# Taking four engines' instructions in the planner's order instead of the build tool's

## The chip, the cores and the metric

The kernel runs on one core of a Trainium2 chip. The metric is the time of one execution on the device in microseconds (us); lower is better. A kernel is timed in several runs, and the median of them is its time.

## What is computed

Two layers of a decoder over 1024 tokens of width 1024 in float32. Layer 0 is "forgetting attention" (FoX): a causal softmax attention whose scores carry a running sum of log forget gates. Layer 1 is native sparse attention (NSA): each query attends to compressed blocks of keys, to the key blocks selected (with this size all causal ones), and to a window of 512 keys, and the three results are summed by gates. Its keys and values are made once from the residual stream behind layer 0. Each layer ends with a feed-forward part with a convolution over three tokens. Cut to that:

```python
def conv_ffn(xn, w_up, conv_w, conv_b, w_down):       # width 1024 -> 2 x 2816 -> 1024
    u = xn @ w_up
    u_pad = jnp.pad(u, ((0, 0), (CONV_W - 1, 0), (0, 0)))
    c = sum((conv_w[j] * u_pad[:, j:j + T] for j in range(CONV_W)), conv_b)
    gate, val = jnp.split(c, 2, axis=-1)
    return (jax.nn.silu(gate) * val) @ w_down

def reference(x, positions, ...):
    h = x
    for layer in range(2):
        if layer == 0:
            h = h + forgetting_attention(rms_norm(h, a_norm[0]), a_w_in[0], ..., a_w_out[0])
        else:
            h = h + native_sparse_attention(rms_norm(h, b_norm[0]), positions, kc, vc, ks, vs, kw, vw, b_w_in[0], ...)
        h = h + conv_ffn(rms_norm(h, f_norm[layer]), f_w_up[layer], f_conv_w[layer], f_conv_b[layer], f_w_down[layer])
        if layer == 0:
            kc, vc, ks, vs, kw, vw = shared_kv(h, positions, kv_norm, kv_w, ...)
    return h
```

## The kernel before

**Products.** Every large matmul is made in three passes over operands that are split into a high part (rounded) and a low part (the remainder): high x high, high x low, low x high (`mm3`, L206 to L212, so nearly all matmuls stand under L210, L211 and L212). ScalarE rounds the high part (L1021 in the FFN, L859 and L216 elsewhere) and VectorE subtracts it from the source for the low part (L1022, shown under its helper L1017). The up and down projections of the FFN are each cut in 2 x 2 blocks and made by Strassen's scheme of seven products with sums of blocks before and after, so VectorE also makes `sum`, `xs`, `u` and `b` (L1017 too).

**Task lists.** Five stretches of the kernel are not written as loops of instructions but as lists of tasks: the FoX attention (`fox_attn`), the FFN of layer 0 and of layer 1 (`ffn`, called twice), the entry of the NSA layer, with keys, values and part of the query projection (`nsa_in`), and the NSA attention (`nsa_attn`). A task names an engine, a duration, a priority (a position `u` plus an offset for its kind), what it comes after and which buffers of which ring it takes. `Flow.run` (L147) plays the engines through with those durations: at each step the task that can start first is taken, by priority among those that can, and its function is called, which emits its instructions. So the order of the instructions in the source is the order of that plan. The input projection of layer 0 and a rest of its output projection are no lists; they stand as written.

**What sets the order that runs.** Each engine runs its instructions in one order. In the kernel before, the build tool orders the instructions of every engine anew by costs of its own, within what data and buffers allow; the plan's order is only where it starts from. The transfers are issued by SyncE (SP), whose queue the tool orders too.

**Lines that the following sections name.** Attention: scores `s` by TensorE (L584, L785, L1895, L1896, L1917, L1920), row maximum `sm` by VectorE (L593, L588), exponential `pt` by ScalarE (L596), scaling by GpSimd (L600), transposes `t` by TensorE (L613), the split of `t` into `p_h` (ScalarE, L624) and `p_l` (VectorE, L626), product with the values `v` (L618, L619), results copied and added into `ot` (L638, L642). The compressed branch of the NSA attention has its own softmax: L1924 (maximum), L1936 (VectorE subtracts it), L1940 (ScalarE exponential), L1928 to L1931 and L1941 (GpSimd scales). The output weights of layer 1 are split by `split_tasks`: L859 (ScalarE, high part) and L860 (GpSimd, low part). Query norms: L1668 (square), L1661 (sums), L235 and L236 (root), L239 to L243 (correction of the root), L1429 (scaling), L1401 to L1406 (rotation, GpSimd), L1678 (transposes), L1685 and L1686 (split). L956 is a square for the norm ahead of the second FFN, made inside the NSA attention. FFN: norm by L1042 (square), L1045 (GpSimd), L1053 (transposes), L1057; then the seven products of each of 22 channel blocks, `snap` (L1152), the convolution by L1198 (ScalarE) and two taps L1197 (VectorE), the gated product L1207, and the down projection. Each finished row of the FFN of layer 0 is normed (`leave`, L2106 to L2119, GpSimd's part L2119) for the NSA layer.

**Rotation tables.** `self.rope` holds sine and cosine for the rotation of keys and queries. For the queries the gain is multiplied into them once: `q_turns` makes four tables `turn_q` with four GpSimd products (L1470), as a task of its own with priority 8, early in the list of `nsa_in`.

Of the kernel before, what the change touches and what calls it, by code (L numbers as in the profile page):

```python
# [6 lines left out]
FT = mybir.dt.float32  # L7
# [3 lines left out]
AF = mybir.ActivationFunctionType  # L11
OP = mybir.AluOpType
# [4 lines left out]
P = 128  # L17
T = 1024
D = 1024
NT = T // P  # L20
# [50 lines left out]
class Ring:  # L71
# [9 lines left out]
    def room(self):  # L81

        rooms = [self.n % len(self.rooms)] if self.turn else range(len(self.rooms))
        c = [(b.free + .2 if b else 0.0, k) for k in rooms for b in [self.rooms[k]] if b is None or not b.left]
        return min(c) if c else (None, None)
# [109 lines left out]
class Trunk:  # L195
    def __init__(self, tc, A):
        self.tc, self.nc, self.A = tc, tc.nc, A

    def pool(self, name, bufs=1, side=None, space=None):
        kw = {"space": space} if space is not None else {}  # L200
        if space is not DRAM:
            kw["reuse_waits"] = "tile"
        return self.tc.tile_pool(name=name, bufs=bufs, side=side, **kw)

# [40 lines left out]
    def rstd_tasks(self, ss, n, inv, scale):  # L245

        st = {}

        def begin():
            st["f"], st["r"] = self.rstd_steps(self.ap_o, ss(), n, inv)  # L250
            st["f"][0]()

        def end():
            st["f"][2]()
            scale(st["r"])
        return [("DVE", .08, "Q", begin), ("ACT", .45, "Q", lambda: st["f"][1]()), ("DVE", .9 if n > 1 else 1.4, "Q", end)]
# [482 lines left out]
    def fox_attn(self, qT, kT, vS, xT, weights, w_room, o_late, wo_steps, early):  # L739
        nc, hp = self.nc, self.hp  # L740
        with ExitStack() as es:
# [3 lines left out]
            F = self.flow  # L745
# [8 lines left out]
            u = 0  # L754
# [65 lines left out]
            F.run()  # L820
# [164 lines left out]
    def ffn(self, layer, xT, first, X, U, rows, g_dram, conv, leave, ahead=None):  # L985
# [11 lines left out]
        with ExitStack() as es:  # L997
            en = es.enter_context
            fp = en(self.pool("ff", 1))
            self.ap_o = en(self.pool("ff_sm", 2))  # L1000
# [33 lines left out]
            def norm(i, n):  # L1034
# [5 lines left out]
                def square():  # L1040
                    st["ss"] = self.ap_o.tile([P, 1], FT, name="nt_ss")
                    nc.scalar.activation(xt.t, x.t, AF.Square, accum_out=st["ss"])  # L1042
                load = F.add("SP", moved(P, D), u, "", lambda: nc.sync.dma_start(x.t, rows[i]), (), [x])
                *steps, last = self.rstd_tasks(lambda: st["ss"], 1, 1.0 / D, lambda r: st.update(r=r))
# [299 lines left out]
            F.run()  # L1344
# [78 lines left out]
    def nsa_in(self, turns, begin, quarters, xT, kv, q_dram, nw):  # L1423
# [6 lines left out]
        with ExitStack() as es:  # L1430
# [30 lines left out]
            turn_q = [cc.tile([P, NT, 8], FT, name=f"turn_q{m}") for m in range(4)]  # L1461
# [6 lines left out]
            def q_turns():  # L1468
                for tq, (t, x) in zip(turn_q, ((1, 0), (0, 1), (1, 1), (0, 0))):
                    nc.gpsimd.tensor_tensor(tq, self.rope[t][:, :NT], gr[:, None, 8 * x:8 * x + 8].to_broadcast([P, NT, 8]), op=OP.mult)  # L1470
# [131 lines left out]
            turns_made = F.add("POOL", 1.5, 8, "", q_turns)  # L1602
# [24 lines left out]
            u = 0  # L1627
# [25 lines left out]


# [58 lines left out]
            F.run()  # L1713
# [150 lines left out]
    def nsa_attn(self, kv, q_dram, late, wo, steps, res, dst, norms, nw):  # L1864
# [3 lines left out]
        with ExitStack() as es:  # L1868
# [149 lines left out]
            F.run()  # L2018
# [3 lines left out]
    def kv_tiles(self, p, U):  # L2022
        ku = U(0, [8, 512], "k_u")
        vu = U(1, [2, 4, G, P], "v_u")
        kv = {"k": [[[[p.tile([P, 512], FR, name=f"k{br}{g}{x}"), ku[:, br * 4 + g * 2 + x]] for x in range(2)]
                     for g in range(G)] for br in range(2)]}
        kv["v"] = [[p.tile([P, 4, G, P], FR, name=f"v{br}"), vu[:, br]] for br in range(2)]
        kv["kc"] = p.tile([P, G, 2, HD], FR, name="kc")
        kv["vc"] = [[p.tile([P, P], FR, name=f"vc{g}{a}") for a in range(2)] for g in range(G)]
        kv["gate"] = p.tile([P, NT, 3 * H], FT, name="gate")  # L2030
        return kv

    def build(self, out):
        A, nc = self.A, self.nc
        with self.pool("const", 1) as cp, self.pool("dram", 1, space=DRAM) as dp, self.pool("w", 3) as self.wp, \
# [70 lines left out]
            def leave(F, i, h, after, u):  # L2106
# [7 lines left out]
                def square():  # L2114
                    st["ss"] = self.ap_o.tile([P, 1], FT, name="nt_ss")
                    nc.scalar.activation(junk.t, h(), AF.Square, accum_out=st["ss"])
                *steps, last = self.rstd_tasks(lambda: st["ss"], 1, 1.0 / D, lambda r: st.update(r=r))
# [106 lines left out]
```

## Time and profile before

| what | us |
|---|---|
| median of 3 runs (lowest, highest) | 2728.29 (2725.96, 2731.55) |
| the profiled execution | 2730.28 |
| its span, first to last instruction | 2728.5 |
| TensorE busy (share of the span) | 2643.6 (97%) |
| VectorE busy | 2138.1 (78%) |
| ScalarE busy | 1511.9 (55%) |
| GpSimd busy | 560.8 (21%) |
| mean granted clock of TensorE | 0.994 |

The stages follow one another nearly without overlap: input projection of layer 0 from 0 to 253, FoX attention to 620, rest of its output projection to 657, first FFN to 1310, entry of the NSA layer to 1486, NSA attention to 2076, second FFN to the end. In the rows below PE is TensorE, DVE is VectorE, ACT is ScalarE, POOL is GpSimd. A row of the timeline gives start and duration in us, engine, line, operation, output and inputs by the program's names, and in brackets the time in which the engine stood idle before it with the instruction that released it. Idle time of an engine other than TensorE costs only what it makes TensorE wait.

### The profile page before, as it was taken

The page shows a single profiled execution, that of the slowest core. Times are in us where ns is not written, and L with a number is a line of the kernel's source. Part 1 is how long each engine was busy: PE and PEld are TensorE (multiplying, and loading weights), DVE is VectorE, ACT ScalarE, POOL GpSimd, SP SyncE. Part 2 cuts the span into 40 slices and gives each one's busy share as a digit, 9 for nine tenths or more (in the row PEclk, how much of TensorE's full clock was granted, in tenths as well). Part 3 has the DMA queues.
Part 4 walks back from the last instruction along what each step waited for, and adds up shares of the span by engine and source line. Part 5 has one row for each costly group of instructions (what it writes and reads, how often), then busy time and mean ns, then how long its engine had stood idle before and what let it go on. Part 6 is the DMA issues. An engine that isn't in the chain of part 4 may idle for free. (4 is left out here: it accounts for less than half of the span.)

```text
span 2728.5 us, 39283 instructions
## 1 busy us (share of the span) xinstructions
PE 2643.6 (97%) x13384; PEld 2174.1 (80%) x13384; DVE 2138.1 (78%) x4012; ACT 1511.9 (55%) x3168; POOL 560.8 (21%) x843
## 2 busy tenths in 40 slices
PE   8999999999999999999999899999999999999999
PEld 6678777787788888888888688887787788888887
DVE  6752778755987787989786788887886987877988
ACT  5332677744655454445754677676776554545443
POOL 1111445410000000000463654444452000000000
PEclk9999999999999999999999899999999999999999
DMA  6474657724332224544224300000113422224553
GB/s 183 110 180 160 173 159 208 188 89 135 120 98 72 93 71 147 214 139 156 90 80 136 109 20 17 28 28 32 63 44 112 136 85 93 77 85 165 189 167 128
DMA packets 277209, 312.42 MB, mean 115 GB/s; under 512 B 19992, under 2 KB 194496, under 8 KB 277008
## 3 DMA queue, kind: packets, MB, share of 16 engines
q1 hardware_dynamic: 277008, 309.90, 37.0%
q8 instruction: 106, 1.74, 0.3%
q14 instruction: 95, 0.78, 0.1%
HBM read 238.41 MB, written 71.43 MB: 114 GB/s over the span
## 5 line engine op out<-in xcount | busy, mean ns | idle before, releaser
L1021 ACT CAST op<-sum 128x512 fp32r<-128x512 f32 x396 | 241.7, 622 | 309.9 <-PE ps L212 200.6
L210 PE MATMUL ps<-xs,op 128*128 128x512 f32 x880 | 344.9, 393 | 7.9 <-ACT snap L1152 5.5
L211 PE MATMUL ps<-xs,op 128*128 128x512 f32 x880 | 344.0, 391 | 0.4 <-DVE xs L1017 0.4
L212 PE MATMUL ps<-xs,op 128*128 128x512 f32 x880 | 342.6, 390 | 0.4 <-DVE op L1017 0.4
L596 ACT ACTIVATE pt<-s,sm 128x640 f32<-128x640 f32 (+7 forms) x384 | 276.1, 723 | 103.0 <-DVE sm L593 44.4
L1017 DVE TENSOR_TENSOR op<-sum,op 128x512 fp32r<-128x512 f32 x396 | 267.1, 688 | 82.9 <-ACT op L1021 82.8
L626 DVE TENSOR_TENSOR p_l<-t,p_h 128x512 fp32r<-128x512 f32 x456 | 277.7, 628 | 45.6 <-ACT p_h L624 42.2
L624 ACT CAST p_h<-t 128x512 fp32r<-128x512 f32 x456 | 237.5, 545 | 97.7 <-PE t L613 94.3
L613 PE MATMUL t<-ident,pt 128*128 128x128 f32 x1632 | 246.9, 276 | 11.4 <-DVE p_l L626 8.5
L600 POOL TENSOR_SCALAR pt<-pt,sm,gate 128x640 f32<-128x640 f32 (+7 forms) x256 | 201.7, 793 | 216.9 <-DVE sm L599 191.4
L211 PE MATMUL ps<-op 128*128 128x512 f32 x616 | 241.0, 391 | 3.8 <-DVE op L1017 3.8
L212 PE MATMUL ps<-op 128*128 128x512 f32 x616 | 239.9, 389 | 0.0
L210 PE MATMUL ps<-op 128*128 128x512 f32 x616 | 235.1, 390 | 0.0
L1197 DVE SCALAR_TENSOR_TENSOR acc<-u,cw,acc 128x1023 f32<-128x1023 f32 (+1 forms) x176 | 225.1, 1281 | 5.4 <-ACT acc L1198 2.8
L593 DVE TENSOR_REDUCE sm<-s 128x1 f32<-128x640 f32 (+7 forms) x256 | 210.6, 834 | 17.7 <-PE s L584 14.7
L613 PEld LDWEIGHTS t<-ident,pt 128*128 128x128 f32 x1632 | 186.6, 142 | 42.4 <-DVE p_l L626 12.0
L210 PEld LDWEIGHTS ps<-xs,op 128*128 128x128 f32 x880 | 165.7, 189 | 47.1 <-ACT snap L1152 6.9
L211 PEld LDWEIGHTS ps<-xs,op 128*128 128x128 f32 x880 | 166.0, 189 | 35.9 <-DVE xs L1017 1.8
L212 PEld LDWEIGHTS ps<-xs,op 128*128 128x128 f32 x880 | 165.8, 188 | 35.7 <-DVE op L1017 1.3
L618 PE MATMUL v<-p_h,v 128*128 128x512 f32 (+1 forms) x376 | 155.6, 416 | 7.8 <-DVE ot L642 4.6
L1152 ACT COPY snap<-ps 128x512 f32<-128x512 f32 x132 | 77.2, 585 | 153.8 <-PE ps L212 153.7
L211 PEld LDWEIGHTS ps<-op 128*128 128x128 f32 x616 | 115.6, 188 | 31.9 <-DVE op L1017 8.3
(467 smaller groups left out, 6398.3 us busy)
## 6 DMA issues: line engine op xcount, KB each, us to landing
w_raw<-in_f_w_up SPq DMA_DIRECT2D x96, 512.0 KB
u<-in_f_w_down SPq DMA_DIRECT2D x176, 256.0 KB
s_g<-acc SPq DMA_DIRECT2D x40, 512.0 KB
g<-s_g SPq DMA_DIRECT2D x20, 1024.0 KB
w_raw<-in_a_w_in SPq DMA_DIRECT2D x32, 512.0 KB
qa<-s_q SPq DMA_DIRECT2D x32, 256.0 KB
ka<-s_k SPq DMA_DIRECT2D x32, 256.0 KB
v<-s_v SPq DMA_DIRECT2D x16, 512.0 KB
```

The costliest lines, as they stand in the source:

```text
L210: mm(out, a[0], b[0], start=start, stop=False, **kw)
L211: mm(out, a[0], b[1], start=False, stop=False, **kw)
L212: mm(out, a[1], b[0], start=False, stop=stop, **kw)
L593: b = a if joint else F.add("DVE", .066 + 1.0417e-3 * n, u, "M", lambda z=z, c=c: nc.vector.tensor_reduce(sm["nm"][:, c], src(ps.t, z), ax ...
L596: e = F.add("ACT", .238 + .8333e-3 * n, u, "E", lambda z=z, c=c, out=out: nc.scalar.activation(out(), src(ps.t, z), AF.Exp, bias=sm["nm"][ ...
L600: ("POOL", .327 + .8333e-3 * n, "N", lambda r=r, c=c, out=out: nc.gpsimd.tensor_scalar(out(), out(), sm["rs"][:, c], gate(r) if gate else ...
L613: nc.tensor.transpose(t.t[:, r * P:(r + 1) * P], b(), self.ident)
L624: h = F.add("ACT", .052 + .8333e-3 * n, u + 1 + x, "H", lambda: nc.scalar.copy(p2.t[0][:, :n], t.t[:, :n]), after=[a], uses=[t, p2])
L626: lambda: nc.vector.tensor_tensor(p2.t[1][:, :n], t.t[:, :n], f32(p2.t[0][:, :n]), op=OP.subtract), after=[h], uses=[t, p2])
L1017: TT = lambda out, a, b, op: nc.vector.tensor_tensor(out, a, b, op=op)
L1021: a = F.add("ACT", .52, u, "", lambda: nc.scalar.copy(op.t[:, 0], src()), after, [op], uses)
L1197: return lambda: nc.vector.scalar_tensor_tensor(acc.t[:, sh:], o.t[:, :T - sh], cw[j][:, c:c + 1], acc.t[:, sh:], op0=OP.mult, op1=OP.add)
```

## The change

Each of the five lists is now run through `Trunk.run`, which wraps `flow.run()` in a manual schedule for four engines: TensorE, ScalarE, VectorE and GpSimd keep the order in which the source emits their instructions. SyncE's transfers are still ordered by the build tool. The small sums and roots of a norm in the FFN list and in `leave` lie in one tile `nt_rs` of five columns from a pool of 6 instead of in separate tiles from a pool of 2. The four query tables no longer have a tile each: two lie in a new tile `turn` beside keys and values, two overwrite the rotation tables in place, and the task that makes them moves from priority 8 to the priority `u` of the list's end, behind all rotations of keys (`rotated`).

```diff
+    def run(self, flow):
+
+        e = mybir.EngineType
+        with self.tc.manual_schedule(engines={e.PE, e.Activation, e.DVE, e.Pool}):
+            flow.run()
...
-    def rstd_tasks(self, ss, n, inv, scale):
+    def rstd_tasks(self, ss, n, inv, scale, room=lambda: None):
...
-            st["f"], st["r"] = self.rstd_steps(self.ap_o, ss(), n, inv)
+            st["f"], st["r"] = self.rstd_steps(self.ap_o, ss(), n, inv, room=room())
...
-            F.run()
+            self.run(F)
...
-            self.ap_o = en(self.pool("ff_sm", 2))
+            self.ap_o = en(self.pool("ff_sm", 6))
...
-                    st["ss"] = self.ap_o.tile([P, 1], FT, name="nt_ss")
-                    nc.scalar.activation(xt.t, x.t, AF.Square, accum_out=st["ss"])
+                    st["rs"] = self.ap_o.tile([P, 5, 1], FT, name="nt_rs")
+                    nc.scalar.activation(xt.t, x.t, AF.Square, accum_out=st["rs"][:, 0])
...
-                *steps, last = self.rstd_tasks(lambda: st["ss"], 1, 1.0 / D, lambda r: st.update(r=r))
+                *steps, last = self.rstd_tasks(lambda: st["rs"][:, 0], 1, 1.0 / D, lambda r: st.update(r=r), lambda: st["rs"][:, 1:])
...
-            turn_q = [cc.tile([P, NT, 8], FT, name=f"turn_q{m}") for m in range(4)]
+            turn_q = [kv["turn"][:, m] for m in range(2)] + [t[:, :NT] for t in self.rope[::-1]]
...
-                for tq, (t, x) in zip(turn_q, ((1, 0), (0, 1), (1, 1), (0, 0))):
-                    nc.gpsimd.tensor_tensor(tq, self.rope[t][:, :NT], gr[:, None, 8 * x:8 * x + 8].to_broadcast([P, NT, 8]), op=OP.mult)
+
+                for m, x in enumerate((0, 1, 1, 0)):
+                    nc.gpsimd.tensor_tensor(turn_q[m], self.rope[(m + 1) % 2][:, :NT], gr[:, None, 8 * x:8 * x + 8].to_broadcast([P, NT, 8]), op=OP.mult)
...
-            turns_made = F.add("POOL", 1.5, 8, "", q_turns)
...
+            turns_made = F.add("POOL", 1.5, u, "", q_turns, rotated)
...
+        kv["turn"] = p.tile([P, 2, NT, 8], FT, name="turn")
```

## Rows read from the trace of the kernel before

**Rows 1.** The page's part 1: busy us of each engine, share of the span, instructions.

```profile
PE 2643.6 (97%) x13384; PEld 2174.1 (80%) x13384; DVE 2138.1 (78%) x4012; ACT 1511.9 (55%) x3168; POOL 560.8 (21%) x843
```

**Rows 2.** Busy us (instructions) by stage: PE, PEld, DVE, ACT, POOL; clock, DMA, GB/s.

```profile
253.30:620.00 366.70, 354.20 (x2034) 287.42 (x2033) 262.99 (x576) 238.53 (x565) 135.30 (x160) 1.00 0.58 163
...
657.00:1310.00 653.00, 641.76 (x2837) 525.45 (x2838) 555.51 (x823) 336.42 (x561) 19.66 (x14) 1.00 0.38 124
1310.00:1486.00 176.00, 170.64 (x924) 153.01 (x923) 129.00 (x416) 105.24 (x339) 85.94 (x267) 1.00 0.37 108
1486.00:2076.00 590.00, 562.78 (x3529) 467.77 (x3528) 480.21 (x1014) 405.84 (x973) 282.20 (x376) 0.98 0.15 45
2076.00:2728.50 652.50, 639.61 (x2805) 524.01 (x2803) 545.28 (x791) 323.58 (x527) 5.30 (x4) 0.99 0.38 126
```

**Rows 3.** Timeline of DVE, NSA attention's head: start, us, operation [idle before].

```profile
1496.40 0.69 DVE L1661 TENSOR_REDUCE w_raw<-w_raw 128x8 f32<-128x512 f32 x1 [1.74 <-ACT w_raw L1668]
...
1511.75 1.22 DVE L593 TENSOR_REDUCE sm<-s 128x1 f32<-128x1024 f32 x1
```

**Rows 4.** Timeline of PE around the same place.

```profile
1485.68 0.47 PE L210 MATMUL t<-w_h,xT 128*128 128x512 f32 x1
...
1491.58 0.66 PE L1678 MATMUL t<-ident,w_raw 128*128 128x128 f32 x4 [1.53 <-POOL w_raw L1406]
...
1514.25 0.80 PE L1895 MATMUL s<-k,q 128*128 128x512 f32 x1 [6.59 <-ACT pt L596]
```

**Rows 5.** Busy time of PE alone in three stretches; then granted clock.

```profile
1510.60:1517.40 6.80, 3.15 (x8) 0.50 0.01 2
1561.80:1568.60 6.80, 5.50 (x18) 0.50 0.25 77
1886.00:1889.40 3.40, 3.35 (x12) 0.50 0.01 2
```

**Rows 6.** Timeline of all engines, 1549 to 1564.

```profile
1550.90 0.50 PE L1895 MATMUL s<-k,q 128*128 128x512 f32 x1 [1.68 <-ACT pt L596]
...
1553.26 7.50 POOL L860 TENSOR_TENSOR wo<-w_raw,wo 128x512 fp32r<-128x512 f32 x6
...
1554.99 6.32 DVE L1936 TENSOR_TENSOR pt<-pt,nmc 128x512 f32<-128x512 f32 x1
...
1563.10 1.12 PE L613 MATMUL t<-ident,pt 128*128 128x128 f32 x4 [3.50 <-DVE p_l L626]
```

**Rows 7.** Timeline of all engines, 1882 to 1887.

```profile
1882.57 1.06 ACT L956 ACTIVATE w_raw<-w_raw 128x1024 f32<-128x1024 f32 x1 [1.54 <-issue]
...
1886.06 0.77 PE L618 MATMUL v<-p_h,v 128*128 128x512 f32 x1 [2.42 <-DVE ot L642]
```

**Rows 8.** Timeline of DVE, first FFN, from up to down projection.

```profile
1082.66 0.69 DVE L1017 TENSOR_TENSOR op<-sum,op 128x512 fp32r<-128x512 f32 x1
1086.23 0.69 DVE L1017 TENSOR_TENSOR u<-ps,snap 128x512 f32<-128x512 f32 x1 [2.88 <-PE ps L212]
...
1090.89 2.60 DVE L1197 SCALAR_TENSOR_TENSOR acc<-u,cw,acc 128x1023 f32<-128x1023 f32 x2 [0.60 <-ACT acc L1198]
...
1094.01 2.60 DVE L1197 SCALAR_TENSOR_TENSOR acc<-u,cw,acc 128x1023 f32<-128x1023 f32 x2
1096.71 1.23 DVE L1207 TENSOR_TENSOR acc<-acc 128x1024 f32<-128x1024 f32 x1
```

**Rows 9.** Timeline of PE at the same place: first and second down product.

```profile
1091.40 0.39 PE L210 MATMUL ps<-op 128*128 128x512 f32 x1
...
1096.88 0.50 PE L210 MATMUL ps<-op 128*128 128x512 f32 x1
```

**Rows 10.** Busy time in the head of the first FFN, columns as in Rows 2.

```profile
675.00:712.00 37.00, 31.64 (x141) 24.18 (x140) 36.45 (x63) 24.34 (x55) 4.26 (x2) 1.00 0.30 92
```

**Rows 11.** Timeline of POOL at the entry of the NSA layer.

```profile
1317.41 2.96 POOL L2119 TENSOR_SCALAR h<-h,rs_r 128x1024 f32<-128x1024 f32 x2 [10.32 <-DVE rs_r L242]
...
1324.33 0.33 POOL L1470 TENSOR_TENSOR turn_q<-rope_cos,g_r 128x64 f32<-128x64 f32 x1
```

More of the change, by code (lines that the diff above doesn't have):

```diff
@@ L1343, in ffn @@
                 ahead(F, u)
-            F.run()
+            self.run(F)
     def rope_tables(self, cp, tp, pp):
@@ L1712, in nsa_in @@
                 pass
-            F.run()
+            self.run(F)
             wq = [(w, []) for w, _ in wq]
@@ L2017, in nsa_attn @@
                         self.norm_tasks(u, *norms(n), n, [early[n], *(uses if n == 7 else ())])
-            F.run()
+            self.run(F)
     def kv_tiles(self, p, U):
@@ L2114, in square @@
                 def square():
-                    st["ss"] = self.ap_o.tile([P, 1], FT, name="nt_ss")
-                    nc.scalar.activation(junk.t, h(), AF.Square, accum_out=st["ss"])
-                *steps, last = self.rstd_tasks(lambda: st["ss"], 1, 1.0 / D, lambda r: st.update(r=r))
+                    st["rs"] = self.ap_o.tile([P, 5, 1], FT, name="nt_rs")
+                    nc.scalar.activation(junk.t, h(), AF.Square, accum_out=st["rs"][:, 0])
+                *steps, last = self.rstd_tasks(lambda: st["rs"][:, 0], 1, 1.0 / D, lambda r: st.update(r=r), lambda: st["rs"][:, 1:])
                 d = F.chain(u, [("ACT", 1.09, "", square), *steps, ("DVE", .4, "", last[3])], [*after, self.after_silu], [junk])
```

## The prediction

> **What bounds the kernel now.** I read the page first: TensorE is busy 2643.6 of 2728.5 us [rows 1], so no other engine bounds the whole, and the change, which neither adds nor takes away a matmul, can only move the 85 us in which TensorE is idle and the few stretches in which its clock is halved. Next the busy time by stage, cut where the task lists begin and end [rows 2]: idle is 366.7 - 354.2 = 12.5 us in the FoX attention, 11.2 in the first FFN, 5.4 in the entry of the NSA layer, 27.2 in the NSA attention and 12.9 in the second FFN with the kernel's end, 69 us in all. That is the ceiling of any gain by reordering, plus half of what the half-clock stretches hold. Last I compared order: the instructions of the kernel before carry numbers in the order of the source, and the trace gives the order in which they ran. On TensorE 302 of 2032 instructions of the FoX list, 203 of 2836 and 110 of 2804 of the FFN lists, 45 of 921 and 343 of 3528 of the two NSA lists ran behind one that the source has later. So the change does move work, in all five lists, and what it is worth is read place by place: where did the tool's order leave TensorE waiting, and where would the source's order make it wait?
>
> The profiled execution took 2730.28 us, 1.8 us more than its span and 2.0 more than the median of 2728.29. The sum is made against it and the difference is added to the median.
>
> **Half clock.** In the three stretches of [rows 5] the granted clock is 0.50, the lower of the two levels (1.2 GHz); busy time in them does half the work. 3.15 busy us in the first cost 1.6, 5.50 in the second cost 2.75, 3.35 in the third cost 1.7. TensorE had waited 6.59 us around the first, 3.50 before and in the second, 2.42 before the third [rows 4, 6, 7]. There are seven such stretches in all; two of the four not shown lie in the head of the second FFN, one each in the FoX attention and, like the third here, beside the wait of 1.68 us [rows 6].
>
> **NSA attention, head (1486 to 1518): gain.** The tool put pieces of the late query norms on VectorE ahead of the row maxima. The pieces wait for ScalarE: VectorE is idle 1.74 us before the first at 1496.40 [rows 3], and two more like it follow. The row maximum `sm` L593, whose scores are finished before these, stood behind them and ran at 1511.75 [rows 3]; the exponential came after it, and TensorE waited 6.59 us for that, until 1514.25 [rows 4]. In source order the maxima stand right behind their scores. Gain 6.59 + 1.6 = 8.2. But TensorE's first task of this list in the source is the transposition of the kept query tile, which ran at 1491.58 behind GpSimd's rotation [rows 4]. Before it the tool had pulled 18 projection matmuls from 1485.68 on [rows 4]; in order TensorE stands idle from 1485.7 to 1491.6, 5.9 us instead of 1.53, loss 4.4, with a stretch of half clock (1.7) or without. Net -3.8 or -2.1; I take **-3**.
>
> **1549 to 1563: gain of unsure size.** The tool put ScalarE's weight splits L859 ahead of an exponential: TensorE waits 1.68 us [rows 6], with a half-clock stretch 1.7 more; in the source the exponential comes first. Then VectorE's L1936, two SBUF inputs, took 6.32 us [rows 6] where an L1017 of the same shape takes 0.69 [rows 8]. It ended 0.6 us after GpSimd had gone through six L860 in a row, 7.50 us from 1553.26 [rows 6]. What waits on L1936 let TensorE idle 3.50 us, and 2.75 went to half clock. All of it gone would be -9.6. The source, however, has four L860 in a row (4 x 1.25 = 5.0) before the task that follows L1936, so a block of about 4.7 us can come back, then up to the price seen now: the bounds are -9.6 and -1.4. I take **-4**, nearer to the second, since the long block is the only row of such a meeting. By the Trainium skill ("SBUF — State Buffer", summary of rules for kernel authors), VectorE with two SBUF inputs and GpSimd reading SBUF exclude each other, and the one that issues second is blocked until the first finishes; taken by the single instruction, that is one L860 of 1.25 us at most, and this place would give about -8 and the whole sum would be 2726. The row of 6.32 us disagrees: the wait went on through the whole row of L860.
>
> **1882 to 1886: gain.** ScalarE's L956 (a Square that waited for a load) ran at 1882.57 after an idle of 1.54 us [rows 7], ahead of a cast and a copy of the attention that needed no load; behind that TensorE waited 2.42 us and lost 1.7 to the clock. In the source the attention steps come first: **-4**. The rest of this list has many waits of 0.3 to 1.1 us that change both ways: 0, bounds -5 and +8.
>
> **FFN, from up to down projection, both layers: loss.** In the source VectorE takes the convolution taps L1197 and the product L1207 of the last channels ahead of the low parts of the first down products. The tool had done these in a gap: `op` at 1082.66, before an idle of 2.88 us [rows 8]. I walk the source's order with durations of rows 8 (taps 1.30 each, L1207 1.14 to the next start, others 0.60) and ready times held: the taps still begin at 1090.89, when ScalarE's part is there, so the low part of the first down product is done at 1094.05. TensorE gets there at 1091.40 [rows 9] and takes it in its second matmul: 2.5 us of wait. Two more taps, L1207, a sum, two low parts: the second product's low part is done at 1100.2, TensorE was there at 1096.88 [rows 9]: 3.4 us. Some of the wait is won back from the waits that it has in the trace, and the fifth product starts 5.1 us later than in the trace. The second layer has the same pattern (its `op` 1420 us later): 5.4. With no half clock the loss is 10.5, with two stretches of 1.7 in each layer 17.3. A wait of 2.42 us had a stretch behind it [rows 5, 7], but these are broken by a product each time, so I count one of the four: **+12**. If VectorE works its backlog off earlier in the up projection, which the held times can't show, the loss is 0.
>
> **FFN heads.** The tool's ScalarE ran the first norm's Square L1042 4 us after it was ready; the source's order lets it go first. But from 675 to 712 VectorE is busy 36.45 of 37.0 us [rows 10], so what comes earlier waits there: -0.5, and -1 for the second layer; bounds -4 and +2 together.
>
> **NSA entry (1310 to 1326): loss.** In the source TensorE waits for the finished rows (GpSimd's L2119, whose first two end at 1320.4 [rows 11]) before products that the tool ran first: +1.7 to +2.5 in the walk, **+2.5** with a chance of half clock.
>
> **FoX attention:** its largest wait (1.6 us at 321.5, for weights that are still being loaded) is in the source's order too; other small moves go both ways: 0, bounds -4 and +3.
>
> **Tables and room.** The query tables' four GpSimd products, 0.33 us each [rows 11], 1.3 us in all, move behind the key rotations, and the first query rotation waits for them and stands behind them on the same queue. GpSimd has 176 - 86 = 90 us free in that stage [rows 2], so 0; if that cover is gone, +1.3. Two of them now overwrite the rows of the rotation tables that only the keys read; the wait for `rotated` is what that needs. More rooms for the norm's small sums remove waits only: 0. The loads keep the tool's order on SP's queue and are not bounded apart: a load that comes late for a moved step would be inside the bounds of the places above.
>
> **Sum:** -3 - 4 - 4 + 12 - 1.5 + 2.5 + 0 = **+2 us**: 2732.3 for an execution like the profiled one, 2730 on the median.
>
> **Rivals.** (1) *VectorE is in time at the down projection.* Then the +12 is absent and the rest stays: -10, that is 2718; with the upper bounds of the second place 2712. For it: VectorE is busy 556 of 653 us in the first FFN [rows 2], so it has spare time; against it: in the walk the taps' start hangs on ScalarE and not on a backlog. (2) *In-order queues stall on their heads.* A wait at the head of VectorE's or ScalarE's queue now holds all behind it, and no ready instruction of another task slips in. Its place is the up-to-down step, 17.3 us with half clock, and the GpSimd rows beside L1936, where the gains of 3 and 4 us don't come: 17.3 + 2.5 - 4 - 1.5 = +14, or with the +3 of the FoX attention +17: 2743 to 2745. It decides from the point at which the NSA gains are under 9 us. (3) *The reorder does little.* With the other engines' times held, TensorE alone in source order ends the five lists later by 0.5, 0.5, 1.7, 0 and 0.8 us, 3.5 together; with gains of the same size the time is 2728. The 1003 displaced instructions speak against no change, but most are displaced without a wait.
>
> **How the numbers follow.** Forecast 2730 (2724 to 2737): chance 0.36. Rival 1, 2718 (2709 to 2724): 0.34. Rival 2, 2744 (2737 to 2753): 0.22. Rival 3, 2728: 0.08. The range leaves out about 1 in 10 at each end: 2709 to 2749. A difference of 0.2%, 5.5 us, is about what a measurement of this kernel can tell from none: faster is below 2722.8, slower above 2733.8. Faster: nearly all of rival 1 and the low end of the forecast, 0.36. Slower: rival 2 and a quarter of the forecast, 0.31. Same: 0.33.
>
> **What would show it.** Right: no wait of over 3 us for `pt` L596 near 1500 to 1515, but one of 5 to 6 us before the first transposition L1678; VectorE's taps directly ahead of the low parts at the end of each up projection, with waits of TensorE for `op` L1017 of 2 to 3.5 us there; no wait of 2.4 us near 1886. Wrong: waits for `op` L1017 that sum to no more than now (then rival 1), or new waits spread over all lists behind ScalarE and VectorE (then rival 2, more widely than I placed it). The forecast falls altogether if the lists' ends shift by more than 10 us in the FoX attention or the middle of an FFN, where I count nothing.

## The result, and the profile after

The changed kernel takes 2770.15 us (median of 4 runs, 2767.72 to 2772.42), the kernel before 2729.57 in the same comparison: a ratio of 1.0148 with a 95% interval of 1.0134 to 1.0161, 40 us slower. The forecast was 2730 with a range of 2709 to 2749, so the time lies outside it. The profiled execution has a span of 2765.9 us.

The page's first part, as in [rows 1]:

```profile
PE 2652.2 (96%) x13384; PEld 2178.6 (79%) x13384; DVE 2151.2 (78%) x4012; ACT 1512.0 (55%) x3168; POOL 553.5 (20%) x843
```

The busy time by stage, cut at the same TensorE instructions as [rows 2] (PE, PEld, DVE, ACT, POOL; clock; DMA; GB/s):

```profile
253.60:628.10 374.50, 354.13 (x2034) 292.10 (x2033) 266.36 (x578) 239.88 (x565) 135.00 (x160) 0.98 0.56 159
665.60:1345.20 679.60, 650.84 (x2837) 527.37 (x2838) 559.49 (x826) 338.77 (x565) 18.05 (x12) 0.99 0.36 119
1345.20:1524.00 178.80, 170.93 (x924) 155.07 (x924) 134.19 (x419) 104.51 (x338) 84.53 (x275) 0.98 0.38 109
1524.00:2093.60 569.60, 555.83 (x3529) 463.91 (x3528) 477.33 (x1007) 403.21 (x969) 278.64 (x370) 1.00 0.15 46
2093.60:2765.90 672.30, 646.18 (x2804) 524.59 (x2802) 549.15 (x791) 323.38 (x527) 4.96 (x4) 0.99 0.37 122
```

TensorE does the same work, 13384 instructions. The stages of [rows 2] went from 366.7 to 374.5 us (FoX attention), 653.0 to 679.6 (first FFN), 176.0 to 178.8 (NSA entry), 590.0 to 569.6 (NSA attention) and 652.5 to 672.3 (second FFN and end). So the NSA attention gained 20 us, and the FFNs' stages lost 27 and 20.

Finer: TensorE executes nearly the same sequence in both kernels, so the start of its n-th instruction in one trace can be set against the n-th in the other. The difference, read at instructions that stand at the given times in the trace of before, grows by:

| stretch (us in before) | predicted | measured |
|---|---|---|
| FoX attention, 253 to 620 | 0 | +7.7 |
| rest of the output projection, to 657 | 0 | +0.5 |
| first FFN, head, to 760 | -0.5 | +6.0 |
| up projection, to 1075 | 0 | **+10.2** |
| step to the down projection, to 1110 | +6 | +5.2 |
| down projection and NSA entry, to 1475 | +2.5 | +2.5 |
| NSA attention, head, to 1549 | -3 | -4.2 |
| to 1575 | -4 | -6.0 |
| to 1860 | 0 | -1.6 |
| to 1905 | -4 | -3.7 |
| to 2060 | 0 | +0.4 |
| second FFN, head, to 2170 | -1 | +4.5 |
| up projection, to 2498 | 0 | **+6.7** |
| step, to 2530 | +6 | +7.2 |
| down projection, to 2720 | 0 | +1.7 |
| sum | +2 | +37.1 |

(The +12 of the two steps is put down as 6 each. The span grew by 37.4 us; the rest lies before 253.) The 2.5 of the row for the down projection and the NSA entry is a sum of three: +3.0 in the down projection, +3.3 at the entry's first products and -3.8 behind them. What TensorE waited for, longest sums, changed kernel (us in total, times, longest):

```profile
PE ps L216 <- DVE op L1022: 12.3, 15, 2.2
PE ps L215 <- ACT xs L1072: 11.9, 4, 5.0
...
PE ps L215 <- DVE u L1022: 7.1, 12, 1.7
...
PE t L618 <- DVE w_raw L706: 6.0, 3, 3.6
PE t L1685 <- POOL w_raw L1411: 5.2, 1, 5.2
```

In the kernel before the first three were 3.8, 1.3 and 0.3 us. They belong to the FFN: the first half to the steps (5.8 us) and for the rest mostly to the down projections, the second to the heads, the third to the up projections.

**Where the up projection loses.** VectorE, one channel block of the first FFN, kernel before:

```profile
982.64 0.68 DVE L1017 TENSOR_TENSOR op<-w_raw,op 128x512 fp32r<-128x512 f32 x1
983.25 1.22 DVE L1207 TENSOR_TENSOR acc<-acc 128x1024 f32<-128x1024 f32 x1
984.38 0.68 DVE L1017 TENSOR_TENSOR u<-ps,snap 128x512 f32<-128x512 f32 x1
984.98 0.68 DVE L1017 TENSOR_TENSOR op<-w_raw,op 128x512 fp32r<-128x512 f32 x1
986.66 0.69 DVE L1017 TENSOR_TENSOR op<-w_raw,op 128x512 fp32r<-128x512 f32 x1 [1.00 <-ACT op L1021]
...
991.07 0.69 DVE L1017 TENSOR_TENSOR sum<-w_raw 128x512 f32<-128x512 f32 x1 [1.00 <-DMA w_raw<-in_f_w_up]
991.68 0.68 DVE L1017 TENSOR_TENSOR u<-ps,snap 128x512 f32<-128x512 f32 x1
```

and the issues of the weight loads on SP there:

```profile
983.36 0.37 SPq L1106 DMA_DIRECT2D w_raw<-in_f_w_up  x1
...
987.38 0.37 SPq L1106 DMA_DIRECT2D w_raw<-in_f_w_up  x1
```

An earlier block of the same projection in the changed kernel, VectorE, then SP, then TensorE:

```profile
883.96 3.80 DVE L1202 SCALAR_TENSOR_TENSOR acc<-u,cw,acc 128x1022 f32<-128x1022 f32 x3
887.86 1.22 DVE L1212 TENSOR_TENSOR acc<-acc 128x1024 f32<-128x1024 f32 x1
889.00 0.68 DVE L1022 TENSOR_TENSOR op<-sum,op 128x512 fp32r<-128x512 f32 x1
889.60 0.68 DVE L1022 TENSOR_TENSOR u<-ps,snap 128x512 f32<-128x512 f32 x1
890.20 1.89 DVE L1022 TENSOR_TENSOR op<-w_raw,op 128x512 fp32r<-128x512 f32 x3
...
898.12 0.69 DVE L1022 TENSOR_TENSOR sum<-w_raw 128x512 f32<-128x512 f32 x1 [3.38 <-DMA w_raw<-in_f_w_up]
898.73 0.69 DVE L1022 TENSOR_TENSOR u<-ps,snap 128x512 f32<-128x512 f32 x1
```

```profile
890.91 1.57 SPq L1111 DMA_DIRECT2D w_raw<-in_f_w_up  x2
```

```profile
899.47 0.50 PE L215 MATMUL ps<-xs,op 128*128 128x512 f32 x1 [1.16 <-DVE u L1022]
```

In the tool's order the low part `op<-w_raw` stands ahead of the gated product (L1207); it is the last reader of a raw weight buffer, and 0.03 us behind it the first load is issued, the second 4 us later. In the source's order four taps (the row shows the last three), the product (now L1212), another low part and a sum come first, and the three low parts of raw weights stand in a row: the loads go out at 890.91 and 892.12, side by side. VectorE then comes to `sum<-w_raw`, which needs the load, and stands idle 3.38 us; at the same place of the sequence it was 1.99 before, and the block shown from before has 2.83 now instead of 1.00. In all it was, before (760 to 1085), 17.4 us, and 40.1 now (the row is with e6):

```profile
DVE sum L1017 <- DMA w_raw<-in_f_w_up: 17.4, 16, 2.0
```

Queued behind `sum<-w_raw` is `u<-ps,snap`, the sum that frees a PSUM bank (the part of TensorE's output memory that the next product needs), which follows without a pause; and TensorE waits 1.16 us for that bank. In the first up projection it waits 12 times in all, 5.7 us, up to 1.67 at once. The other 4.5 us of the 10.2 are no idle time in the trace. A product lasts 0.39 us and the next starts 0.23 us after it, so the first 0.16 us of a delay show no idle time, and the start behind a late product comes 0.34 us after it instead of 0.23. With 16 late places, four of them without idle time, that is about 4 us.

**The step to the down projection** came where it was predicted. VectorE, then TensorE, first FFN of the changed kernel:

```profile
1115.58 2.60 DVE L1202 SCALAR_TENSOR_TENSOR acc<-u,cw,acc 128x1023 f32<-128x1023 f32 x2 [0.71 <-ACT acc L1203]
1118.10 0.68 DVE L1022 TENSOR_TENSOR op<-sum,op 128x512 fp32r<-128x512 f32 x1
1118.70 2.59 DVE L1202 SCALAR_TENSOR_TENSOR acc<-u,cw,acc 128x1023 f32<-128x1023 f32 x2
1121.40 1.23 DVE L1212 TENSOR_TENSOR acc<-acc 128x1024 f32<-128x1024 f32 x1
1122.55 0.69 DVE L1022 TENSOR_TENSOR sum<-u,b 128x512 f32<-128x512 f32 x1
...
1124.35 0.69 DVE L1022 TENSOR_TENSOR op<-sum,op 128x512 fp32r<-128x512 f32 x1
```

```profile
1118.84 0.59 PE L216 MATMUL ps<-op 128*128 128x512 f32 x1 [2.23 <-DVE op L1022]
...
1123.94 0.50 PE L215 MATMUL ps<-op 128*128 128x512 f32 x1 [0.72 <-ACT op L1026]
1125.09 0.50 PE L216 MATMUL ps<-op 128*128 128x512 f32 x1 [0.65 <-DVE op L1022]
```

```profile
1119.10:1122.50 3.40, 3.40 (x9) 2.63 (x9) 3.26 (x3) 1.76 (x4) 0.00 (x0) 0.50 0.92 339
```

The first down product's low part stands behind two taps and TensorE waits 2.23 us for it (2.5 predicted); the second product's sum, cast and low part stand behind two more taps and the product: 0.72 and 0.65 us. A stretch at the lower clock, 0.50, of 3.4 us from 1119.1 on, all busy (the last view, columns as in [rows 2]), costs 1.7. Behind the second product's two waits TensorE has fallen 6.0 us further behind the trace of before; the walk, which counts from the same times, had 3.4 there. By 1110 the step's growth is 5.2. The second layer's step has such a stretch too, at 2549.3.

**The NSA attention** came as predicted too. Its first transposition:

```profile
1523.48 1.12 PE L1685 MATMUL t<-ident,w_raw 128*128 128x128 f32 x4 [5.17 <-POOL w_raw L1411]
```

It waits 5.17 us in place of the 1.53 of [rows 4] (5.9 predicted); the wait of 6.59 us behind it is gone, and so is the wait of 2.42 us of [rows 7]. The subtraction that took 6.32 us in [rows 6], now L1943, over all of its 16 executions (shortest, median, longest ns):

```profile
L1943 DVE TENSOR_TENSOR pt<-pt,nmc x16: 672/692/1418, 1533.9 to 2062.5; 128x512 f32<-128x512 f32 x16
```

**The heads.** Where TensorE waited 2.64 us at 706 before, it now waits longer:

```profile
717.75 0.79 PE L215 MATMUL ps<-xs,op 128*128 128x512 f32 x1 [4.98 <-ACT xs L1072]
```

The cast that it waits for had itself waited for VectorE's `b`:

```profile
717.08 1.22 ACT L1072 CAST xs<-b 128x512 fp32r<-128x512 f32 x2 [0.69 <-DVE b L1022]
```

VectorE went on without a pause around it, as before [rows 10]; that its order alone decides what is late is not shown (e4). A stretch of half clock lies around the wait, another 2.5 us:

```profile
716.30:723.10 6.80, 4.98 (x11) 3.61 (x12) 6.80 (x12) 1.93 (x4) 0.00 (x0) 0.50 0.78 243
```

**The FoX attention.** TensorE's busy time there is the same, 354.13 us against 354.20; its idle time grew from 12.5 to 20.4 us, and the trace has four stretches of half clock there instead of one.

### The profile page after: what moved, and what is told of

The parts are those of the page before. It is cut to its first block, busy times and chain, and to the rows that moved or that the text cites. A ratio compares the mean times of both kernels' runs of the same rounds, so it can differ in the third digit from the quotient of the medians.

```text
span 2765.9 us, 39310 instructions
## 1 busy us (share of the span) xinstructions
PE 2652.2 (96%) x13384; PEld 2178.6 (79%) x13384; DVE 2151.2 (78%) x4012; ACT 1512.0 (55%) x3168; POOL 553.5 (20%) x843
## 4 chain that ended last, share of the span: by engine, by line
PE 58%; DVE 25%; DMA 6%; issue 5%; ACT 4%; POOL 0%; SPq 0%; DVEq 0%; ACTq 0%; POOLq 0%
PE ps L216 8%; PE ps L217 8%; PE ps L215 8%; DVE op L1022 6%; PE t L618 5%; DMA w_raw<-in_f_w_up 5%; DVE acc L1202 4%; DVE sum L1022 4%; PE v L623 3%; PE v L624 3%; PE ps_m L217 3%; PE ps_m L215 3%; PE ps_m L216 3%; PE t L215 2%; PE t L217 2%
## 5 line engine op out<-in xcount | busy, mean ns | idle before, releaser
L216 PE MATMUL ps<-op 128*128 128x512 f32 x616 | 242.7, 394 | 12.3 <-DVE op L1022 12.3
L215 PE MATMUL ps<-op 128*128 128x512 f32 x616 | 241.5, 392 | 3.0 <-ACT op L1026 3.0
L217 PE MATMUL ps<-op 128*128 128x512 f32 x616 | 241.2, 392 | 0.0
L1203 ACT ACTIVATE acc<-u,cb,cw 128x1024 f32<-128x1024 f32 x88 | 109.6, 1245 | 74.1 <-DVE u L1022 72.3
```

The costliest lines, as they stand in the source:

```text
L215: mm(out, a[0], b[0], start=start, stop=False, **kw)
L216: mm(out, a[0], b[1], start=False, stop=False, **kw)
L217: mm(out, a[1], b[0], start=False, stop=stop, **kw)
```

## The experiments

Each is compared with the kernel before, run beside it on the same chip (2729 to 2731 us there). "Fixed" is an engine that keeps the source's order in a list. Growths of stretches come from the one profiled execution, which can lie off the median (e5 +7.9 us, e4 -5.8, e12 -5.1, e2 +4.6).

**e1, tables only.** All four `self.run(F)` back to `F.run()`:

```diff
-            self.run(F)
+            F.run()
```

> The changed kernel with all five lists left to the build tool's order: only the tables, the rooms of the norm's sums and the later table task remain. Theory (the order alone costs and gains): 2729.6 +- 3 us, no difference from before. Rival (the moved table task or the shared sums take part in the loss): over 2735.

Measured: 2725.4 us, ratio 0.9977 (0.9968 to 0.9987): 5 to 6 us faster than before, so neither case. The gain lies in the NSA attention, -8.6 us from 1475 to 2060 and -7.6 of it before 1549: with the tables and rooms changed (which of the two, no run separates) the tool ordered the head of that list differently, and the wait of 6.59 us didn't come. From 1480 to 1520 TensorE's longest wait is the 1.53 us for the kept tile:

```profile
1492.91 0.66 PE L1685 MATMUL t<-ident,w_raw 128*128 128x128 f32 x4 [1.53 <-POOL w_raw L1411]
```

So more than half of the 15 us that the changed kernel gains there against before could be had in the tool's order too. The source's order alone costs some 45 us in the changed kernel.

**e2, NSA attention alone in source order** (the other three calls as in e1).

> Only the list of the NSA attention keeps the source's order. Between the two traces this stage went from 590.0 to 569.6 us. Theory (each list's gain or loss is its own): 2729.6 - 20 = 2709, and the following FFN as before. Rival (the stage is shorter only because the entry of the layer left its 5.2 us wait and its displaced products elsewhere, or the later FFN gives it back): 2718 or more.

Measured: 2718.0 us, ratio 0.9949 (0.9932 to 0.9965). The rival's time: the stage itself is as short as in the changed kernel (569.8 us), but ahead of it stands the wait for the kept tile, 5.6 us.

**e3, the three attention lists in source order**, the FFN lists the tool's (`F.run()` in `ffn` alone).

> FoX attention, NSA entry and NSA attention keep the source's order, both FFN lists are the tool's. From the stages of the two traces: 2729.6 + 7.7 + 2.7 - 20.4 = 2720. If the lists work on one another, another time: over 2728 when the FFN's head suffers from what the attention leaves, under 2712 when the FoX list's loss came from its neighbour.

Measured: 2728.3 us, ratio 0.9989 (0.9980 to 0.9998). That is 3 us faster than before, not the 10 expected. The second FFN is back (648.5 us to TensorE's last product, 648.6 before). The first takes 657.0, so it keeps 4 of its 27 us though its list is the tool's; they arise in the last 30 us ahead of the cut, right before the fixed list of the NSA entry. The FoX list costs 9.9 here and not 7.7; in the seven traces with this list fixed on all four engines it cost 7.7 to 11.1. So the FFN lists make the loss, some 43 us of it, and the FoX list eats a large part of what the NSA list gains.

**e4, VectorE left to the tool in the FFN lists**, everything else fixed:

```diff
-        with self.tc.manual_schedule(engines={e.PE, e.Activation, e.DVE, e.Pool}):
+        with self.tc.manual_schedule(engines={e.PE, e.Activation, e.DVE, e.Pool} - set(free)):
...
-            self.run(F)
+            self.run(F, {mybir.EngineType.DVE})
```

> All five lists in source order, but in the two FFN lists VectorE is left to the build tool. Theory (VectorE's order in the FFN, taps ahead of the low parts that free the raw weights and of the sums that free the banks, makes the loss of 47 us there): most of it goes, 2770 - 35 = 2735 or less. Rival (TensorE's or ScalarE's fixed order makes it): 2760 or more.

Measured: 2752.2 us, ratio 1.0075 (1.0057 to 1.0093), between the two. The drift of the up projections is gone (+0.5 and +0.7 instead of +10.2 and +6.7), but the steps still cost 5.6 and 4.5, the heads 2.8 and 5.4. So VectorE's order is needed for the drift, and it is not the whole of the rest.

**e5, VectorE and ScalarE left to the tool in the FFN lists.**

> All five lists in source order, but in the FFN lists VectorE and ScalarE are both left to the build tool; TensorE and GpSimd stay fixed. With VectorE alone left free the drift of the up projection was gone, but the step from up to down projection still cost 6.5 and 4.5 us and the heads 3 to 5. Theory (ScalarE's order, its casts for the down projection behind the convolution's first part, makes those too): the FFN stages come to 657 + 650 us, the whole to 2728 +- 3, as with the FFN lists left to the tool. Rival (TensorE's fixed order makes the step and the heads): 2740 or more.

Measured: 2734.1 us, ratio 1.0017 (1.0007 to 1.0026); FFN stages 660.3 and 657.0 us. Steps 1.9 and 2.9, heads 1.5 and 1.7, drift none. The theory holds for most. Left over e3 are 3 us in the first and 8 in the second FFN, 4.2 of them in the second down projection; by the medians, with the profiled execution the slowest of ten, 7 us in all. TensorE and GpSimd are the engines still fixed; which of them makes it, no run shows.

**e14, ScalarE alone left to the tool in the FFN lists.**

> All five lists in source order, ScalarE alone left to the tool in the FFN lists (e4 left VectorE alone: FFN stages 665.4 and 660.3 us; e5 both: 660.3 and 657.0; all fixed 679.7 and 668.7; the tool 653.0 and 648.6). Theory (VectorE's order makes the drift of the up projections and the step to the down projection; ScalarE only follows): the drift stays at 10 and 7 us, the step at 6, the whole at 2763 or more. Rival (the casts on ScalarE are what sets VectorE's late parts): the drift halves or more, 2755 or less.

Measured: 2775.1 us, ratio 1.0172 (1.0157 to 1.0187): drift 9.0 and 8.5, steps 8.0 and 8.2, heads 6.5 and 5.7. The theory holds: with VectorE fixed, freeing ScalarE gives nothing; with VectorE free (e4), ScalarE's fixed order is enough for most of the steps and of the second head, and for half of the first head. Either of the two in the source's order makes most of those, only VectorE's makes the drift.

**e6, half loads.** The order of every instruction stays; each load of up weights is cut in half, and the second half of a weight tile is replaced by the first, so the up projection isn't the reference's.

```diff
-                t = F.add("SP", moved(P, D), u, "", lambda: nc.sync.dma_start(view(), w_up[:, c0:c0 + P].rearrange("(k p) f -> p k f", p=P)), takes=[raw])
+                t = F.add("SP", moved(P, D), u, "", lambda: nc.sync.dma_start(view()[:, :4], w_up[:512, c0:c0 + P].rearrange("(k p) f -> p k f", p=P)), takes=[raw])
...
-                blk = {A11: lambda: v0()[:, :4], A12: lambda: v0()[:, 4:], "A21": lambda: v1()[:, :4], A22: lambda: v1()[:, 4:]}
+                blk = {A11: lambda: v0()[:, :4], A12: lambda: v0()[:, :4], "A21": lambda: v1()[:, :4], A22: lambda: v1()[:, :4]}
```

> The changed kernel, every instruction in the same order, but each load of up weights brings 256 KB instead of 512 (half of the rows; the first half of the weights is used in place of the second). Theory (in the up projection TensorE waits because VectorE's next sum stands at the head of its queue for a load that starts too late, and the sum that frees a PSUM bank is queued behind it): the drift of 10 and 7 us in the two up projections goes, 2770 - 17 = 2753, up to 4 more or less. Rival (VectorE's own order of taps and sums is what comes late, loads or not): 2767 or more.

Measured: 2749.0 us, ratio 1.0071 (1.0056 to 1.0086). Both drifts are gone (-0.1 and -0.5), the steps stay (5.4 and 5.6). What VectorE waited for in the first up projection, changed kernel (from 760 to 1100), then half loads (760 to 1090):

```profile
DVE sum L1022 <- DMA w_raw<-in_f_w_up: 40.1, 16, 3.9
```

```profile
DVE sum L1022 <- DMA w_raw<-in_f_w_up: 4.9, 14, 1.1
```

With the load in time VectorE's order does TensorE no harm there: the drift is the load's lateness, passed on through VectorE's queue.

**e9, the product later.** One number of the plan, so that a low part of raw weights comes ahead of the gated product in the source:

```diff
-                a = F.add("DVE", 1.15, u, "", lambda: nc.vector.tensor_tensor(ga.t, ga.t, acc.t, op=OP.mult), [a, made], uses=[ga, acc])
+                a = F.add("DVE", 1.15, u + 12, "", lambda: nc.vector.tensor_tensor(ga.t, ga.t, acc.t, op=OP.mult), [a, made], uses=[ga, acc])
```

> The changed kernel, all five lists in source order, with one number of the plan changed: the gated product of the FFN gets a priority 12 positions later, so that in the source two low parts stand ahead of it on VectorE, one of them the part that frees the first raw weight buffer. Loads are whole. Theory (the late release of that buffer delays the weight loads, and with them VectorE's next sum and the sum that frees a bank): the drift of the up projections, 10 and 7 us, goes: 2770 - 17 = 2753; the heads and most of the step to the down projection stay. Rival (the loads are late for another reason, such as the stores that stand ahead of them on SP's queue): 2765 or more.

Measured: 2755.6 us, ratio 1.0090 (1.0074 to 1.0107). Drift 1.8 and 1.1, steps 6.0 and 5.9. The longest wait of VectorE for a weight load is down from 3.9 to 2.0 us, the longest of the kernel before:

```profile
DVE sum L1022 <- DMA w_raw<-in_f_w_up: 21.4, 16, 2.0
```

With whole loads and VectorE in source order, two low parts of 0.68 us put ahead of the product give back some 14 us of the whole time. So the first load's start, set by the low part's place on VectorE, is the cause of most of the drift: 14 of its 17 us are gone.

**e7, the kept tile later.** As e2, and in the plan the transposition may not start before 6.5 us:

```diff
                 a = F.add("PE", .44, u, "S", turn, after, [ps], rooms)
+                a.ready = 0.0 if after else 6.5
```

> As e2 (NSA attention alone in source order), and the transposition of the kept query tile may not start before 6.5 us in the plan, so that the plan puts projection products ahead of it. In e2 TensorE waits 5.64 us there. Theory: that wait goes and nothing takes its place, 2718 - 5 = 2713. Rival (the products that go first only move the same wait to their own norms or to the first scores): 2717 or more.

Measured: 2712.3 us, ratio 0.9938 (0.9921 to 0.9955), the lowest median of all: faster than both kernels, 58 us less than the changed one. Its interval overlaps that of e2; the gain over e2 is read from the trace. Span and clock of the profiled execution:

```profile
core 0: 2706.8 us, clock 0.997
```

The wait is gone (entry to 1486: 0.0 instead of +5.8), and nothing came in its place (-11.5 up to 1549).

**e8, e10, e11, e12, e13, the FoX list.** As e3, with one engine of the FoX list left to the tool, or all but TensorE: the set in `self.run(F, {...})` of `fox_attn` is `DVE`, `Activation`, `Pool`, the three of them, and `PE`.

> As e3 (FoX attention, NSA entry, NSA attention in source order, FFN the tool's), but VectorE is left to the tool in the FoX list. That list took 376.7 us in e3 and 366.8 before. Theory (VectorE's order makes the FoX loss, norm pieces that wait for ScalarE ahead of the splits TensorE needs): 367 to 370 us there, 2720 in all. Rival (ScalarE's casts that wait for loads, or GpSimd's row of low parts, make it): 375 us or more, 2727.

> As e3, but ScalarE is left to the tool in the FoX list (376.7 us there in e3, 366.8 before; with VectorE free 375.2). Theory (ScalarE's splits of weights that still load stand ahead of casts and exponentials): 370 us or less, 2721 in all. Rival (GpSimd's low parts L865 next to VectorE's norm pieces make it): 375 us, 2727.

> As e3, but GpSimd is left to the tool in the FoX list. In the source's order its L865 ran beside VectorE's norm pieces L245 to L247, which then took 1.14 to 1.19 us instead of 0.17, and TensorE waited 3.65 and 2.04 us behind them. Theory (that meeting makes the loss): 370 us or less there, 2721 in all. Rival (ScalarE's order, or TensorE's): 375 us, 2727.

> As e3, but in the FoX list only TensorE keeps the source's order. Theory (TensorE's order costs little, the other engines make the loss together, none alone): 367 to 370 us there, 2719. Rival (TensorE's order makes it): 375 us or more, 2727.

> As e3, but in the FoX list TensorE is left to the tool and ScalarE, VectorE and GpSimd keep the source's order. The list took 366.8 us before, 376.7 with all four fixed, 375.2, 372.2 and 373.9 with VectorE, ScalarE or GpSimd free, 376.6 with TensorE alone fixed. Theory (TensorE's order is the larger part of the loss: it stands at a transposition whose PSUM tile a norm still reads): 370 us or less, 2722. Rival (each engine's fixed order is enough to make it): 374 us or more, 2727.

| left to the tool in the FoX list | growth of the stage, us | whole, us | ratio (95%) |
|---|---|---|---|
| none (e3) | 9.9 | 2728.3 | 0.9989 (0.9980 to 0.9998) |
| VectorE (e8) | 8.4 | 2725.4 | 0.9986 (0.9976 to 0.9995) |
| ScalarE (e10) | 5.4 | 2721.4 | 0.9971 (0.9960 to 0.9982) |
| GpSimd (e11) | 7.1 | 2724.3 | 0.9978 (0.9968 to 0.9988) |
| VectorE, ScalarE, GpSimd (e12) | 9.8 | 2729.8 | 0.9997 (0.9987 to 1.0006) |
| TensorE (e13) | 4.6 | 2722.2 | 0.9973 (0.9964 to 0.9983) |

Against the 7.7 to 11.1 us of the same list fixed on all four, only the rows with ScalarE or TensorE free stand clearly lower. VectorE alone and GpSimd alone are not it. TensorE's order alone is enough for the whole loss, and with TensorE free the other three still make half: the list has no one culprit. The largest single wait, changed kernel, GpSimd, VectorE and TensorE:

```profile
449.64 2.49 POOL L865 TENSOR_TENSOR wo_l<-w_raw,wo_h 128x512 fp32r<-128x512 f32 x2
```

```profile
449.60 0.16 DVE L244 TENSOR_TENSOR rs_t<-rs_y 128x8 f32<-128x8 f32 x1
449.79 1.14 DVE L245 TENSOR_TENSOR rs_t<-rs_t,rs_v 128x8 f32<-128x8 f32 x1
450.96 1.19 DVE L246 TENSOR_SCALAR rs_t<-rs_t 128x8 f32<-128x8 f32 x1
452.19 0.17 DVE L247 TENSOR_TENSOR rs_r<-rs_y,rs_t 128x8 f32<-128x8 f32 x1
452.39 0.69 DVE L706 TENSOR_TENSOR w_raw<-t,rs_r 128x512 f32<-128x512 f32 x1
```

```profile
453.14 0.33 PE L618 MATMUL t<-ident,pt 128*128 128x128 f32 x1 [3.65 <-DVE w_raw L706]
```

TensorE has a transposition into the tile that a norm's L706 still reads; L706 stands behind four small steps, of which two lasted until one of GpSimd's two L865 had ended. In the kernel before TensorE had other products first. With GpSimd free (e11) the wait there is still 3.55 us, with VectorE free 3.49, with ScalarE free 3.66, with TensorE free 4.00: it isn't decided by the place of any one engine's work, and what would move it stays open.

## Why the prediction was wrong

**Bounds and places.** That TensorE's waits must be read place by place held; the ceiling was one on gains and says nothing of a loss. The places that were walked came out: the two steps 12.4 us for +12, the head of the NSA attention -4.2 for -3, the second place -6.0 for -4, the third -3.7 for -4. Two matches are luck in part. The steps hold two stretches of half clock, 3.4 us, where one of 1.7 was counted, and 9.0 us without them where 10.5 were walked. The down projection with the NSA entry has 2.5 for +2.5, but only the entry's first products were walked, and they cost 3.3; the rest of the row cancels. Two sums do not come out of their terms, with little effect on the forecast: by the walk's own durations the second product's low part is done at 1099.6, not 1100.2, and the second place's bound of -1.4 comes out at -3.4, the 1.68 and 1.7 that stay when the price of the long block comes back whole.

**The step that failed** is the list of places. It held only those where the trace of before shows TensorE waiting, plus the ones where the first tasks of a list stand in another order; the middle of the up projections, where TensorE waits for nothing in before, got a 0, without a walk of one block. There the new order had the same fault as the step that I did walk: taps and product ahead of the low parts. I saw it at the end of the up projection and not that it repeats in every block, because I followed the low part to its TensorE product only, which has time to spare, and not to the raw weight buffer that it frees, the load that waits for this buffer, and the next sum that waits for the load. The sentence that SP's loads were "not bounded apart" left out that price: 10.2 + 6.7 us (e4, e6 and e9 show the cause). It is the largest part of the 35 us by which the traces miss the forecast; the heads are 12 of it, the FoX attention with the rest of its projection 8, and the NSA attention gained 4 more than forecast.

**The heads** were put at -0.5 and -1 with a bound of +2 for both. They cost 6.0 and 4.5. That VectorE is busy through [rows 10] was read as "what comes earlier waits there"; an instruction that the new order puts ahead on a full engine also delays another, and TensorE's wait of 4.98 us stands behind a cast that waited for VectorE. With VectorE and ScalarE free they cost 1.5 and 1.7 (e5).

**The FoX attention** had 0 with an upper bound of +3 and cost 7.7 (9.9 in e3). The bound came from the one wait that I looked at. With 302 of 2032 the list had the largest share of displaced instructions on TensorE and was not walked; the count alone would have given no bound either, for 343 displaced ones in the NSA attention went with a gain. What makes the loss there stays open (e8, e10 to e13).

**The rivals.** Rival 2 named the mechanism, queues that stall on their heads, but only at the places already walked, and its 2744 was 26 us too low. The sign by which the forecast was to fall, more than 10 us in the middle of an FFN, is what came. Rival 1 failed on its own condition, VectorE in time at the down projection: the steps cost 12.4 us. That e2 and e7 end near its 2718 is no support for it, since they leave the FFN lists to the tool.

**The tables and rooms** were put at 0. Their own instructions cost nothing that shows, but with them the tool's order of the next list changed, which gave 6 us (e1). That was no case of the prediction, and it is no part of the changed kernel's time in the lists, where the order is fixed.

## What to carry to other kernels

An order that is to be fixed should be walked through one full period of the steady stretch too, and each displaced instruction followed to everything it releases: the buffer, the load that waits for that buffer, and what is queued behind the consumer of the load. Fix the order by list, not for all at once: here the NSA attention gained 20 us and the two FFN lists lost some 43, and a version with only the first fixed, with one late start put into the plan, is 0.6% faster than before (0.2% of it comes with the tables and rooms alone, e1).

## What the runs showed of the hardware

In the changed kernel a VectorE instruction that met GpSimd's work lasted until one GpSimd instruction ended: L245 1.14 us at 449.8, L246, which has one input only, 1.19 us at 451.0, and L1943 at most 1.42. In the kernel before one such meeting lasted through the rest of a row of six, 6.32 us [rows 6], and in the tool's order of e1 it came again at the same place:

```profile
1547.03 7.47 POOL L865 TENSOR_TENSOR wo<-w_raw,wo 128x512 fp32r<-128x512 f32 x6
...
1548.54 6.51 DVE L1943 TENSOR_TENSOR pt<-pt,nmc 128x512 f32<-128x512 f32 x1
```

By the Trainium skill ("SBUF — State Buffer", summary of rules for kernel authors), when VectorE has two SBUF inputs and GpSimd reads SBUF, the one that issues second is blocked until the first finishes. L245 and L1943 of the changed kernel agree, the two long rows don't, and no run here says why. The place where the forecast set the rule against the row gave -6.0 us in the changed kernel, between the -4 of the row and the -8 of the rule, and less than 0.2 either way in e1, where the long row stayed.

In the first up projection of the kernel before, 14 of 16 pairs of weight loads of 512 KB were issued 3.1 to 4.0 us apart, and the sum that waits for them started 3.7 to 4.7 us behind the second issue; behind the other two pairs, 1.2 us apart, it was 5.1. In the changed kernel all pairs were issued 1.2 us apart, and the sum started 4.8 to 6.0 us behind the second. So a load with another close ahead of it is in later; that the two share what the transfers can move fits this, but no run separates it.
